# Reordering around a triangular substitution: weight splits, a norm's root, two loads and two stores

## The chip, the cores and the metric

The kernel runs on one core of a Trainium2 chip. A core has five engines, each with its own in-order instruction stream: TensorE (PE, matmuls), VectorE (DVE), ScalarE (ACT), GpSimd (POOL) and SyncE (SP, which here only issues DMAs). ACT issues DMAs too, between its own instructions. An instruction that waits holds everything behind it on its engine. The metric is the device time of one execution in microseconds (us); smaller is better.

## The reference, cut to what matters

One layer of a diffusion backbone over 1024 latent and 256 context tokens of width 1024. One input projection feeds two mixers: a neighbourhood attention of 8 heads, and a bidirectional chunked gated delta rule of 4 heads of width 128. Both are gated, concatenated and projected out.

```python
h = rmsnorm(x, g_pre) * (1.0 + scale[:, None]) + shift[:, None]
na_q, na_k, na_v, na_z, g_qkv, g_z, g_b, g_a = jnp.split(h @ w_in, IN_SPLITS, axis=-1)
o_na = neighborhood_attention(heads(na_q), heads(na_k), heads(na_v), heads(na_kc), heads(na_vc), rpb)
q, k, v = gdn_qkv(g_qkv, conv_w)                        # short conv, silu, l2norm of q and k
q, k = axial_rope(q, rope), axial_rope(k, rope)
...
a = jnp.where(pos[:, None] > pos[None, :], jnp.einsum('nbhid,nbhjd->nbhij', kb, k) * decay, 0.0)
t_inv = lax.linalg.triangular_solve(eye + a, jnp.broadcast_to(eye, a.shape),
                                    left_side=True, lower=True, unit_diagonal=True)
u = jnp.einsum('nbhij,nbhje->nbhie', t_inv, v * beta[..., None])
...
y = jnp.concatenate([o_na * jax.nn.silu(na_z), o_g * jax.nn.silu(g_z)], axis=-1) @ w_out
x = x + gate[:, None] * rmsnorm(y, g_post)
```

What the change touches is the part between: the delta rule needs, for each head, direction and chunk, the inverse of a unit triangular matrix (`t_inv`), and keys that are l2-normalised and rotated.

## The kernel before, in words

Precision: a projection is done as three matmuls for each 128-row block of the weights. A weight tile is loaded raw (`wr`), cast by ACT to a rounded high half (`wh`, L585), and the low half is the difference (`wl`, L586, on POOL, or on DVE where the tile is one of four parts and its first block is not a multiple of four). PE then does high times high, high times low and low times high (L603, L607, L608 for the form with channels as rows; L616 to L618 for the values of the attention, tiles `pv`). So PE needs `wl` a few matmuls after `wh`. The weights of the attention's values come in four parts, `nv0_0`, `nv0_2`, `nv0_4` and `nv0_6`.

Stages: up to about 75 us normalisation and the first weights; to about 430 us the convolutions and projections of the delta heads h = 0 to 3, with the projections of the attention filled in between them; to about 525 us the rest of the projections together with the merging of triangular inverses; then attention and the delta scan side by side to about 757 us; then the output projection. The program is emitted by Python generators that are stepped in turn, and a list scheduler orders the instructions of each engine; `self.order(r, name)` (L199) adds an edge without a semaphore that pins r behind another instruction of that order.

For each delta head, `qk_tok` turns q and k of the head to tokens on PE (tiles `tp`), squares them on ACT with a sum (`sq`, L1068), takes the root of the keys' sums on POOL (`rsqrt`, L216: an addition and a power, tile `rq_y_g`), scales the keys with it on DVE (`tok`, L1074) and rotates: the queries' rotary products and their sum on POOL, the keys' on DVE (L1084 to L1086). `qk_back` transposes the result back (tiles `tb`), and `delta_front` multiplies keys with keys and queries (tiles `pk`), masks on DVE and POOL (`pm`, `qe`) and stores both (`pm_dram`, `qe_dram`). A 32x32 diagonal block of the result is copied to `ab_dram` for the inversion. A second root on POOL, `rq_y_rho`, belongs to the queries and is read only in the scan.

The inverses are built in two steps. The 32x32 blocks are inverted by substitution on DVE, in the rounds m = 30 to 1 of `inv_pairs` (L1230 to L1235): each round is a product of two parts of `ab` into `tb` (L1233) and an addition back into `ab` (L1235), over 120 partitions and 2m(31-m) elements each. `inv_pairs` takes the 240 blocks of heads 0 to 2 and is stepped from the loop over the head h = 3; the last 80 blocks go through `inv_blocks` later (`ab_vv`, `tb_qh`). At the end `inv_pairs` writes the two inverses to `yd0` and `yd1` (L1241). `inv_merge` (L1266) then combines 32x32 blocks to 128x128: it loads the block factors from memory (`pmf`, L1272, two loads a head of 480 KB) and the inverted blocks (`vl`, L1285, four loads a head of 80 KB), transposes the blocks on DVE (`vx`, `vd`, `ld`, L1291 to L1293), and multiplies on PE (`tz` from `ld` and `pmf`, L1305; `tu` from ACT's copy of `tz`, L1324). Meanwhile PE has projections of the attention to do: `pq` and `pk` of head pairs 2 and 3 (`na_proj`), whose result goes to memory as a high and a low half (`sh`, `sl`, `qk_out`, both stored through SP, L680 and L681), and gates `pz` (`gate_proj`), finished by DVE (`st_z`, L704). `pq`, `pk`, `pz` and `pv` share three PSUM buffers.

## Time and profile before

| | |
|---|---|
| Three timed runs | 854.83, 853.98 and 848.80 us, median 853.98 |
| Profiled execution | 848.82 us, of which the span of the trace is 847.1; 1.7 lies around it |
| PE busy | 814.2 us, 96% of the span, mean granted clock 0.99 |
| DVE, ACT, POOL busy | 495.0 (58%), 418.0 (49%), 365.5 (43%) |
| DMA | 159.67 MB, mean 188 GB/s; SP's queue 54.0% of 16 engines' span, ACT's 5.5% |

PE is the engine to look at: nearly everything else lies beside it. So the time is PE's work plus the few places where PE stands still, and those places are read from the list of waits, from the timeline around them, and from a table of 20 us windows with PE's busy time and the clock granted to it. The profiled execution is the shortest of those known; the other two timed ones are about 5 to 6 us longer.

### The profile page before, as it was taken

The page shows a single profiled execution, that of the slowest core. Times are in us where ns is not written, and L with a number is a line of the kernel's source. Part 1 is how long each engine was busy: PE and PEld are TensorE (multiplying, and loading weights), DVE is VectorE, ACT ScalarE, POOL GpSimd, SP SyncE. Part 2 cuts the span into 40 slices and gives each one's busy share as a digit, 9 for nine tenths or more (in the row PEclk, how much of TensorE's full clock was granted, in tenths as well). Part 3 has the DMA queues.
Part 4 walks back from the last instruction along what each step waited for, and adds up shares of the span by engine and source line. Part 5 has one row for each costly group of instructions (what it writes and reads, how often), then busy time and mean ns, then how long its engine had stood idle before and what let it go on. Part 6 is the DMA issues. An engine that isn't in the chain of part 4 may idle for free.

```text
span 847.1 us, 16613 instructions
## 1 busy us (share of the span) xinstructions
PE 814.2 (96%) x6170; PEld 695.3 (82%) x6170; DVE 495.0 (58%) x988; ACT 418.0 (49%) x1097; POOL 365.5 (43%) x436
## 2 busy tenths in 40 slices
PE   8999999999999999988997999899999999999996
PEld 6688887888788878878985787799898989878885
DVE  4673455546456757699926955556566565743342
ACT  4472525654564664643214334566666666753211
POOL 0042221363482572555452103565757567835121
PEclk9999999999999999999998999999999999999999
DMA  9986442254626626733688579996967923234261
GB/s 332 341 305 213 136 138 90 79 180 161 162 75 227 197 69 230 218 110 102 202 241 239 166 223 293 392 306 181 313 186 257 250 97 128 87 125 137 99 199 50
DMA packets 86343, 159.67 MB, mean 188 GB/s; under 512 B 18405, under 2 KB 45750, under 8 KB 84086
## 3 DMA queue, kind: packets, MB, share of 16 engines
q1 hardware_dynamic: 78774, 144.94, 54.0%
q10 hardware_dynamic: 7488, 13.67, 5.5%
q8 instruction: 49, 0.80, 0.4%
q14 instruction: 32, 0.26, 0.1%
HBM read 109.51 MB, written 52.42 MB: 191 GB/s over the span
## 4 chain that ended last, share of the span: by engine, by line
PE 76%; DMA 9%; DVE 7%; POOL 3%; issue 2%; ACT 2%; SPq 0%; DVEq 0%; POOLq 0%; ACTq 0%
PE py L1550 4%; PE py L1552 3%; PE py L1551 3%; PE pz L607 3%; PE pz L608 3%; PE pz L603 3%; PE pa L1437 3%; DMA vl<-yd 2%; PE po L942 2%; PE po L937 2%; PE tr L926 2%; PE sc L905 2%; PE pa L1422 2%; PE pv L618 2%; PE pv L617 2%; PE pv L616 2%
## 5 line engine op out<-in xcount | busy, mean ns | idle before, releaser
L909 DVE CUSTOM_DVE_ANT_0 pt<-sc,gm 128x544 f32<-128x544 f32 (+1 forms) x64 | 49.4, 772 | 32.3 <-PE sc L905 28.6
L910 ACT ACTIVATE pt<-pt,nm 128x544 f32<-128x544 f32 (+1 forms) x64 | 50.5, 789 | 31.1 <-DVE nm L909 30.7
L893 POOL TENSOR_TENSOR gm<-gt,mk 128x288 f32<-128x288 f32 (+1 forms) x48 | 46.5, 972 | 21.8 <-DVE nm L909 18.6
L1412 POOL TENSOR_SCALAR kd<-kt,kd 128x128 f32<-128x128 f32 x72 | 42.7, 604 | 18.7 <-PE pa L1451 18.2
L1040 DVE SCALAR_TENSOR_TENSOR acc_v<-xp_v,cols,acc_v 128x1282 f32<-128x1282 f32 x16 | 33.1, 2068 | 26.9 <-ACT acc_v L1038 26.6
L1193 POOL TENSOR_SCALAR_AFFINE_SELECT qe<-qe 128x256 f32<-128x256 f32 x32 | 29.0, 907 | 39.8 <-DVE qe L1192 39.8
L1616 DVE TENSOR_TENSOR finv<-py,ggb 128x512 f32<-128x512 f32 (+1 forms) x17 | 10.7, 656 | 51.4 <-ACT finv L1615 43.0
L603 PE MATMUL pz<-hh,wh_gz 128*128 128x512 f32 x96 | 38.9, 405 | 0.0
L607 PE MATMUL pz<-hl,wh_gz 128*128 128x512 f32 x96 | 38.8, 405 | 0.0
L608 PE MATMUL pz<-hh,wl_gz 128*128 128x512 f32 x96 | 38.8, 404 | 0.0
L1174 ACT ACTIVATE em<-em,gc 128x128 f32<-128x128 f32 x80 | 25.5, 390 | 25.7 <-DMA em<-gc_dram 22.9
L618 PE MATMUL pv<-wl_nv,hh 128*128 128x264 f32 x104 | 30.5, 296 | 4.8 <-DVE wl_nv L586 4.8
L1189 DVE SCALAR_TENSOR_TENSOR pm<-pk,nsc,em 128x128 f32<-128x128 f32 x80 | 23.5, 342 | 18.5 <-PE pk L1182 14.6
L1418 POOL TENSOR_SCALAR vb<-v,beta 128x128 f32<-128x128 f32 x40 | 24.2, 606 | 23.0 <-DVE y L1424 13.1
L586 POOL TENSOR_TENSOR wl_gz<-wr_gz,wh_gz 128x512 fp32r<-128x512 f32 x12 | 15.5, 1290 | 37.3 <-ACT wh_gz L585 35.8
L926 PE MATMUL tr<-c,pt 128*96 128x128 f32 (+1 forms) x192 | 31.4, 273 | 0.0
L1454 DVE SCALAR_TENSOR_TENSOR s<-s,egl,pa 128x128 f32<-128x128 f32 x64 | 19.4, 342 | 20.1 <-PE pa L1451 20.1
L924 ACT COPY tcx<-tc 128x256 f32<-128x256 f32 x64 | 23.5, 367 | 15.1 <-PE tc L919 14.5
L928 ACT COPY tl<-tr 96x384 f32<-96x384 f32 (+1 forms) x64 | 30.5, 476 | 0.0
L617 PE MATMUL pv<-wh_nv,hl 128*128 128x264 f32 x104 | 30.0, 291 | 0.0
L616 PE MATMUL pv<-wh_nv,hh 128*128 128x264 f32 x104 | 29.2, 292 | 0.0
L1615 ACT ACTIVATE finv<-py 128x512 f32<-128x512 f32 x14 | 8.3, 598 | 38.7 <-PE py L1552 20.5
(469 smaller groups left out, 2859.3 us busy)
## 6 DMA issues: line engine op xcount, KB each, us to landing
wada<-in_w_ada SPq DMA_DIRECT2D x16, 512.0 KB
em<-gc_dram SPq DMA_DIRECT2D x20, 256.0 KB
pm_dram<-pm SPq DMA_DIRECT2D x20, 256.0 KB
tm_dram<-tm SPq DMA_DIRECT2D x8, 640.0 KB
kk<-qk_dram SPq DMA_DIRECT2D x16, 320.0 KB
tm<-tm_dram SPq DMA_DIRECT2D x4, 1280.0 KB
kq_dram<-kq SPq DMA_DIRECT2D x4, 1152.0 KB
kq<-kq_dram SPq DMA_DIRECT2D x4, 1152.0 KB
```

The lines of the kernel that those rows point to most:

```text
L603: r = nc.tensor.matmul(ps, wh, xh, start=(k == 0 and first), stop=False)
L607: nc.tensor.matmul(ps, wh, xl, start=False, stop=False)
L608: nc.tensor.matmul(ps, wl, xh, start=False, stop=(k == KC - 1))
L616: nc.tensor.matmul(ps, xh, wh, start=(k == 0), stop=False)
L617: nc.tensor.matmul(ps, xl, wh, start=False, stop=False)
L618: nc.tensor.matmul(ps, xh, wl, start=False, stop=(k == KC - 1))
L893: r = nc.gpsimd.tensor_tensor(self.gm[hh][:, 384 - n:384].rearrange("p (n c r) -> p n c r", c=nco, r=4), gv, self.mk[:, mo:mo + n].rearran ...
L909: nc.vector.tensor_tensor_reduce(pt[:, 384 - n:], sc[:, 512 - n:768], gm[:, 384 - n:], -1.0, 3.0e38, ALU.add, ALU.min, nm)
L910: self.last_exp = nc.scalar.activation(pt[:, 384 - n:], pt[:, 384 - n:], AF.Exp, bias=nm, scale=-1.0, accum_out=sums[:, ct, hh:hh + 1]).in ...
L926: self.pe(nc.tensor.transpose(pl[:m, rc * P:(rc + 1) * P], pt[:, 384 + (rc - 3) * m:384 + (rc - 2) * m], self.ident))
L1412: r = nc.gpsimd.tensor_scalar(kd[d], kt_[:, t, :], self.kd[:, h, d, t:t + 1], None, ALU.mult)
L1550: nc.tensor.matmul(py, mh[:, tt], wh[:, nn], start=(k == W_ORDER[0]), stop=False)
```

## The change

Six edits, all in the stretch between about 365 and 470 us.

1. `load_w`: of a weight in four parts, the third part's low half (`wl_nv0_4`) goes from POOL to DVE. The last low half and the last `st_z` are remembered by name.
2. `inv_pairs`: round m = 27 is ordered behind the last of those low halves and the last `st_z`; round m = 26 behind the last scaling of the keys of head 3 (`self.scaled`). In the loop over heads, the rounds' generator is not stepped at the fourth to sixth letter of a head's string.
3. `qk_tok`: for h = 3 the queries' two rotary sums on POOL are put off until the root of the keys is done, and are ordered behind it. The root `rho` is ordered behind the keys' root as well.
4. `inv_merge`: the loads of `vl` are issued ahead of those of `pmf`, and `pmf` is ordered behind them.
5. `qk_out`: for the head pairs 2 and 3 the high halves are stored through ACT's queue.
6. The names that the orders need are recorded (`last_root`, `split`, `gated`, `scaled`).

```diff
@@ rsqrt
-    def rsqrt(self, pool, x, n, tag, eps):
+    def rsqrt(self, pool, x, n, tag, eps, after=None):
         y = pool.tile([P, n], F32, name=f"rq_y_{tag}", tag=f"rq_y{n}")
-        self.nc.gpsimd.tensor_scalar(y, x, eps, None, ALU.add)
-        self.nc.gpsimd.tensor_tensor(y, y, bc(self.mhalf, [P, n]), ALU.pow)
+        r = self.nc.gpsimd.tensor_scalar(y, x, eps, None, ALU.add)
+        if after:
+            self.order(r, after)
+        self.last_root = self.nc.gpsimd.tensor_tensor(y, y, bc(self.mhalf, [P, n]), ALU.pow).ins.name
@@ load_w
-                (nc.vector if halves > 2 and k0 % 4 else nc.gpsimd).tensor_tensor(lo, raw, hi.bitcast(F32), ALU.subtract)
+                r = (nc.vector if halves > 2 and k0 else nc.gpsimd).tensor_tensor(lo, raw, hi.bitcast(F32), ALU.subtract)
+                self.split = r.ins.name
@@ qk_out
-        nc.sync.dma_start(self.qk_dram[0, rows, c0:c0 + n], hi.bitcast(F32))
+        (nc.scalar if p > 1 else nc.sync).dma_start(self.qk_dram[0, rows, c0:c0 + n], hi.bitcast(F32))
         nc.sync.dma_start(self.qk_dram[1, rows, c0:c0 + n], lo.bitcast(F32))
@@ gate_proj
-            nc.vector.scalar_tensor_tensor(z, z, 1.0, pz, ALU.add, ALU.mult)
+            self.gated = nc.vector.scalar_tensor_tensor(z, z, 1.0, pz, ALU.add, ALU.mult).ins.name
@@ the loop over the heads
-                for c in ("RVpppTUpB", "RppVTpUBp", "RVTpUpB", "VRppTppUB")[h]:
+                for j, c in enumerate(("RVpppTUpB", "RppVTpUBp", "RVTpUpB", "VRppTppUB")[h]):
                     step(h, c)
-                    next(blocks, None)
+                    if j < 3 or j > 5:
+                        next(blocks, None)
@@ qk_tok
             r = None if which else self.rsqrt(cv, ss, m, f"g{h}", 4 * EPS)
+            if not which:
+                for tok, rot in late:
+                    self.order(nc.gpsimd.tensor_tensor(tok, tok, rot, ALU.add), self.last_root)
...
-                    nc.vector.tensor_tensor(tok[:, :n, :], pt[:, :n, :],
-                                            bc(r[:, t0 - first:t0 - first + n].unsqueeze(2), [P, n, P]), ALU.mult)
+                    self.scaled = nc.vector.tensor_tensor(tok[:, :n, :], pt[:, :n, :],
+                                            bc(r[:, t0 - first:t0 - first + n].unsqueeze(2), [P, n, P]), ALU.mult).ins.name
...
-                    eng.tensor_tensor(tok, tok, rot, ALU.add)
+                    if which and h == 3:
+                        late.append((tok, rot))
+                    else:
+                        eng.tensor_tensor(tok, tok, rot, ALU.add)
@@ inv_pairs
+            if m == 26:
+                self.order(r, self.scaled)
+            if m == 27:
+                self.order(r, self.split)
+                self.order(r, self.gated)
@@ inv_merge
-            nc.sync.dma_start(pm[d][0:96], self.pm_dram[h][0:96, d])
...
-            nc.sync.dma_start(vl[32 * b:32 * b + 20], self.yd[g][10 * i:10 * i + 20].rearrange("t j i -> t (j i)"))
+            r = nc.sync.dma_start(vl[32 * b:32 * b + 20], self.yd[g][10 * i:10 * i + 20].rearrange("t j i -> t (j i)"))
+        for d in range(2):
+            self.order(nc.sync.dma_start(pm[d][0:96], self.pm_dram[h][0:96, d]), r.ins.name)
@@ delta_load
-            self.rho = self.rsqrt(self.cp, self.ssq.rearrange("p h t -> p (h t)"), 32, "rho", 4 * EPS)
+            self.rho = self.rsqrt(self.cp, self.ssq.rearrange("p h t -> p (h t)"), 32, "rho", 4 * EPS, self.last_root)
```

The edits move instructions, and the scheduler moves others in consequence. On DVE, in the first rounds of `inv_pairs`, before (each pair of rows that writes `tb` and then `ab` is one round; 120x216 is m = 27, 120x260 m = 26, 120x336 m = 24):

```order
239 L1233 TENSOR_TENSOR tb_3501<-ab_3500 120x216
240 L704 SCALAR_TENSOR_TENSOR st_z10_3608<-st_z10_3608,pz1_0_3583 128x512
241 L1235 TENSOR_TENSOR ab_3500<-ab_3500,tb_3501 120x2x27x4
242 L1233 TENSOR_TENSOR tb_3501<-ab_3500 120x260
243 L1235 TENSOR_TENSOR ab_3500<-ab_3500,tb_3501 120x2x26x5
244 L1233 TENSOR_TENSOR tb_3501<-ab_3500 120x300
245 L1235 TENSOR_TENSOR ab_3500<-ab_3500,tb_3501 120x2x25x6
246 L1233 TENSOR_TENSOR tb_3501<-ab_3500 120x336
247 L1235 TENSOR_TENSOR ab_3500<-ab_3500,tb_3501 120x2x24x7
248 L586 TENSOR_TENSOR wl_nv0_6_3762<-wr_nv0_6_3760,wh_nv0_6_3761 128x528
```

and the same place now (`tok3_0` are the keys of head 3, `rq_y_g3` their root):

```order
239 L707 SCALAR_TENSOR_TENSOR st_z10_3608<-st_z10_3608,pz1_0_3583 128x512
240 L588 TENSOR_TENSOR wl_nv0_4_3744<-wr_nv0_4_3742,wh_nv0_4_3743 128x528
241 L588 TENSOR_TENSOR wl_nv0_6_3750<-wr_nv0_6_3748,wh_nv0_6_3749 128x528
242 L707 SCALAR_TENSOR_TENSOR st_z11_3726<-st_z11_3726,pz1_1_3701 128x512
243 L1243 TENSOR_TENSOR tb_3501<-ab_3500 120x216
244 L1250 TENSOR_TENSOR ab_3500<-ab_3500,tb_3501 120x2x27x4
245 L1081 TENSOR_TENSOR tok3_0_0_3652<-tp3_0_0_3649,rq_y_g3_3685 128x256
246 L1081 TENSOR_TENSOR tok3_0_2_3662<-tp3_0_2_3657,rq_y_g3_3685 128x512
247 L1081 TENSOR_TENSOR tok3_0_6_3676<-tp3_0_6_3671,rq_y_g3_3685 128x512
248 L1243 TENSOR_TENSOR tb_3501<-ab_3500 120x260
```

The low half `wl_nv0_6` now stands ahead of round m = 27 and not behind m = 24; the keys' scaling, which stood behind the fifteen rounds m = 30 to 16, stands ahead of m = 26. The rounds m = 26 to 16 come behind it now. On DVE's later rows, `sl_q20`, `sl_q21` and `sl_k22`, which stood behind the last round, now stand between the last seven rounds.

On SP, from the end of head 3's front to the loads of `inv_merge`, before:

```order
218 L1200 DMA ab_dram_94<-pm_dram3_76 32x20x32 x4
219 L1241 DMA yd0_4029<-ab_3500 120x1024
220 L1241 DMA yd1_4031<-ab_3500 120x1024
221 L680 DMA qk_dram_93<-sh_q20_4303 128x512
222 L681 DMA qk_dram_93<-sl_q20_4304 128x512
223 L680 DMA qk_dram_93<-sh_q21_4385 128x512
224 L1209 DMA ab_vv_4309<-ab_dram_94 80x1024
225 L1272 DMA pmf0_0_4330<-pm_dram0_73 96x1280
226 L1272 DMA pmf0_1_4332<-pm_dram0_73 96x1280
227 L1285 DMA vl0_4334<-yd0_4029 20x1024 x4
```

and now:

```order
219 L1210 DMA ab_dram_94<-pm_dram3_76 32x20x32 x4
220 L684 DMA qk_dram_93<-sl_q20_4304 128x512
221 L684 DMA qk_dram_93<-sl_q21_4386 128x512
222 L684 DMA qk_dram_93<-sl_k22_4463 128x256
223 L1256 DMA yd0_4029<-ab_3500 120x1024
224 L1256 DMA yd1_4031<-ab_3500 120x1024
225 L1219 DMA ab_vv_4309<-ab_dram_94 80x1024
226 L684 DMA qk_dram_93<-sl_k20_4579 128x512
227 L205 DMA mk_4586<-in_masks 128x1920
228 L1299 DMA vl0_4332<-yd0_4029 20x1024 x4
229 L1301 DMA pmf0_0_4330<-pm_dram0_73 96x1280
230 L1301 DMA pmf0_1_4331<-pm_dram0_73 96x1280
```

Between `yd1` and `vl0` stood three stores of halves, `ab_vv` and both `pmf`; now `ab_vv`, one store of a half and the load of a mask (`mk`), and `pmf` follows `vl0`. On PE the first `tz` stood in the middle of `pz2_0` and now stands 20 matmuls of 512 columns later, in the middle of `pz2_1`.

On POOL, around the roots, before:

```order
140 L586 TENSOR_TENSOR wl_nv0_4_3756<-wr_nv0_4_3754,wh_nv0_4_3755 128x528
141 L1085 TENSOR_TENSOR tok3_1_6_3636<-tok3_1_6_3636,rope_1138 128x512
142 L218 TENSOR_SCALAR rq_y_rho_5542<-ssq_1140 128x32
143 L1086 TENSOR_TENSOR tok3_1_2_3621<-tok3_1_2_3621,rot3_12_3646 128x512
144 L1086 TENSOR_TENSOR tok3_1_6_3636<-tok3_1_6_3636,rot3_16_3650 128x512
145 L219 TENSOR_TENSOR rq_y_rho_5542<-rq_y_rho_5542,mhalf_67 128x32
146 L218 TENSOR_SCALAR rq_y_g3_3691<-ss3_3654 128x10
147 L1372 TENSOR_TENSOR rho2_5545<-rq_y_rho_5542 128x32
148 L219 TENSOR_TENSOR rq_y_g3_3691<-rq_y_g3_3691,mhalf_67 128x10
```

and now:

```order
140 L1092 TENSOR_TENSOR tok3_1_6_3632<-tok3_1_6_3632,rope_1138 128x512
141 L218 TENSOR_SCALAR rq_y_g3_3685<-ss3_3648 128x10
142 L221 TENSOR_TENSOR rq_y_g3_3685<-rq_y_g3_3685,mhalf_67 128x10
143 L1078 TENSOR_TENSOR tok3_1_2_3617<-tok3_1_2_3617,rot3_12_3642 128x512
144 L1078 TENSOR_TENSOR tok3_1_6_3632<-tok3_1_6_3632,rot3_16_3645 128x512
145 L218 TENSOR_SCALAR rq_y_rho_5542<-ssq_1140 128x32
146 L221 TENSOR_TENSOR rq_y_rho_5542<-rq_y_rho_5542,mhalf_67 128x32
```

The keys' root now follows the queries' rotary products directly, ahead of the queries' sums and of `rho`.

More of the change, by code (lines that the diff above doesn't have):

```diff
@@ L1052, in qk_tok @@
         nc, col = self.nc, self.col
-        toks = []
+        toks, late = [], []
         for which, acc in ((1, qa), (0, ka)):
@@ L1232, in inv_pairs @@
             t3 = tb[:, :2 * m * n].rearrange("p (g a b) -> p g a b", g=2, a=m)
-            nc.vector.tensor_tensor(t3, bc(ab[:, :, 0:m, m:m + 1], [120, 2, m, n]), bc(ab[:, :, m:m + 1, m + 1:], [120, 2, m, n]),
-                                    ALU.mult)
+            r = nc.vector.tensor_tensor(t3, bc(ab[:, :, 0:m, m:m + 1], [120, 2, m, n]),
+                                        bc(ab[:, :, m:m + 1, m + 1:], [120, 2, m, n]), ALU.mult)
+            if m == 26:
[3 more added lines that the diff above has]
+                self.order(r, self.gated)
             nc.vector.tensor_tensor(ab[:, :, 0:m, m + 1:], ab[:, :, 0:m, m + 1:], t3, ALU.add)
```

## The prediction

> **What bounds the kernel now.** PE is busy for 96% of the span, so I read first the list of waits of PE, to see where it is not. All of its waits together are some 25 us, and two of them stand out:
>
> ```profile
> PE tz L1305 <- DVE ld L1293: 5.6, 1, 5.6
> PE pv L618 <- DVE wl_nv L586: 4.8, 1, 4.8
> ```
>
> (the columns are total, times, longest). Both lie where the change is made; all others are below 2.5 us in sum and lie where the order is unchanged. So I read the timeline of PE around both. The first:
>
> ```profile
> 378.98 0.28 PE L616 MATMUL pv<-wh_nv,hh 128*128 128x264 f32 x1
> 379.10 0.28 PE L617 MATMUL pv<-wh_nv,hl 128*128 128x264 f32 x1
> 384.22 0.59 PE L618 MATMUL pv<-wl_nv,hh 128*128 128x264 f32 x1 [4.84 <-DVE wl_nv L586]
> 384.60 0.42 PE L616 MATMUL pv<-wh_nv,hh 128*128 128x264 f32 x1
> 384.82 0.42 PE L617 MATMUL pv<-wh_nv,hl 128*128 128x264 f32 x1
> ```
>
> PE stands for 4.84 us. Then the matmuls follow each other by 0.22 us and not by 0.12: the clock has fallen. Some 13 matmuls run so (until about 387.0), which is another 13 x 0.10 = 1.3 us. Gap one costs 6.1 us. The second:
>
> ```profile
> 447.11 0.40 PE L608 MATMUL pz<-hh,wl_gz 128*128 128x512 f32 x1
> 447.35 0.40 PE L603 MATMUL pz<-hh,wh_gz 128*128 128x512 f32 x1
> 453.32 2.34 PE L1305 MATMUL tz<-ld,pmf 32*32 32x32 f32 x80 [5.58 <-DVE ld L1293]
> ```
>
> and the table of windows behind it (after PE's, PEld's, DVE's, ACT's and POOL's busy time: granted clock, DMA share, GB/s):
>
> ```profile
> 456.00:458.00 2.00, 2.00 (x6) 1.52 (x6) 2.00 (x4) 1.36 (x3) 0.00 (x0) 0.50 1.03 358
> 458.00:460.00 2.00, 2.00 (x9) 1.58 (x8) 1.82 (x4) 1.97 (x6) 1.38 (x1) 0.79 0.86 262
> ```
>
> PE stands 5.58 us and then runs at half clock until about 458.7, so (458.7 - 453.3) / 2 = 2.7 us are lost besides. Gap two costs 8.3 us. Both gaps together, 14.4 us, are all that this change can win.
>
> Why gap one: the timeline of DVE.
>
> ```profile
> 380.06 0.47 DVE L1235 TENSOR_TENSOR ab<-ab,tb 120x300 f32<-120x300 f32 x1
> 380.57 1.45 DVE L1233 TENSOR_TENSOR tb<-ab 120x336 f32<-120x336 f32 x1
> 382.05 1.45 DVE L1235 TENSOR_TENSOR ab<-ab,tb 120x336 f32<-120x336 f32 x1
> 383.43 0.74 DVE L586 TENSOR_TENSOR wl_nv<-wr_nv,wh_nv 128x528 fp32r<-128x528 f32 x1
> ```
>
> The low half that PE wants stands behind substitution rounds, and these take 1.45 us where POOL works on its rotary products and sums and 0.47 where it does not.
>
> **The change part by part.** *Low halves ahead of the rounds.* How early can `wl_nv0_6` be made? ACT's timeline has its cast, and an ACT that is held later:
>
> ```profile
> 376.69 0.63 ACT L585 CAST wh_nv<-wr_nv 128x528 fp32r<-128x528 f32 x1
> ...
> 384.58 0.28 ACT L1068 ACTIVATE sq<-tp 128x128 f32<-128x128 f32 x1 [5.47 <-DVE wl_nv L586]
> ...
> 387.15 0.20 ACT L1068 ACTIVATION_READ_ACCUMULATOR sq<-tp 128x1 f32 x1
> ```
>
> The cast ends at 377.3, the subtraction takes 0.74: 378.1, or 378.8 if `wl_nv0_4`, which DVE takes over, runs late. PE needs it at 379.3. So gap one goes, -6.1, with 0.5 to 1.2 us of cover; each us beyond that comes back. In its place PE's transposes of the rotated keys stand some 60 rows earlier and can wait for DVE. No row shows this; the bounds are 0 and the 3 us by which the rope of the keys can be late, and I take +1.0.
>
> *The rounds wait for the keys' root.* ACT's squares stand behind the load of `wr_nk`, which waits for `wl_nv0_6`; they start at about 379.0 and not at 384.58, and need 387.35 - 384.58 = 2.8 us: 381.8. The root then takes POOL this long:
>
> ```profile
> 389.51 2.45 POOL L219 TENSOR_TENSOR rq_y_g<-rq_y_g,mhalf 128x10 f32<-128x10 f32 x1
> ```
>
> so DVE can scale at 381.8 + 0.3 + 2.45 = 384.5, after having stood idle for some 4 us with round m = 26 behind it. From there I count to the end of the rounds by what DVE did before:
>
> ```profile
> 385.70 0.57 DVE L1233 TENSOR_TENSOR tb<-ab 120x396 f32<-120x396 f32 x1
> ...
> 394.83 1.01 DVE L1074 TENSOR_TENSOR tok<-tp,rq_y_g 128x256 f32<-128x256 f32 x2
> ...
> 426.26 0.22 DVE L1235 TENSOR_TENSOR ab<-ab,tb 120x60 f32<-120x60 f32 x1
> ```
>
> From the scaling to the end of the last round were 426.5 - 394.8 = 31.7 us, with rounds 15 to 1. Now rounds 26 to 16 come on top: 22 to 16 took 394.8 - 385.7 = 9.1, and 26 to 23 are eight operations between 0.47 and 0.57, 4.1. With `sl_q20`, `sl_q21` and `sl_k22` pushed in (two of 0.7, one of 0.4) that is 31.7 + 9.1 + 4.1 + 1.8 = 46.7. End: 384.5 + 46.7 = 431.2, if POOL hinders no round more than before. It can: its two late sums, two more of the four subtractions for `nq2` and `nk2`, and both for `gz2` now fall beside rounds. Each can cost a round 1.45 - 0.47 = 1.0: up to 6, thus 437.2. But not every meeting does:
>
> ```profile
> 415.73 1.70 POOL L586 TENSOR_TENSOR wl_nq<-wr_nq,wh_nq 128x512 fp32r<-128x512 f32 x1 [0.24 <-ACT wh_nq L585]
> 415.77 0.50 DVE L1235 TENSOR_TENSOR ab<-ab,tb 120x336 f32<-120x336 f32 x1
> ```
>
> Here the round kept its 0.50. I take a third, 2: the rounds end at E = 433, 6.5 us later than before, within 431 and 437. [...]
>
> *The loads.* What came behind the rounds before:
>
> ```profile
> 428.75 2.60 SPq L1200 DMA_DIRECT2D ab_dram<-pm_dram  x4
> 431.45 1.15 SPq L1241 DMA_DIRECT2D yd<-ab  x2
> ```
> ```profile
> 449.82 1.25 DVE L1291 STREAM_TRANSPOSE vx<-vl 128x1024 f32<-128x1024 f32 x1 [5.39 <-DMA vl<-yd]
> ```
>
> `yd` went out 5 us behind the rounds' end, since SP stood at the copies to `ab_dram`, which wait for the last `qe` and `pm`. Those are now made many rounds earlier, so `yd` goes out at E + 0.3. From its issue to the landing of `vl` passed 449.7 - 431.5 = 18.3 us. What SP moved in that time, by size:
>
> ```profile
> pmf<-pm_dram SPq DMA_DIRECT2D x4, 480.0 KB
> yd<-ab SPq DMA_DIRECT2D x2, 480.0 KB
> vl<-yd SPq DMA_DIRECT2D x12, 80.0 KB
> qk_dram<-sh_q SPq DMA_DIRECT2D x2, 256.0 KB
> ...
> mk<-in_masks SPq DMA_DIRECT2D x1, 480.0 KB
> ab_vv<-ab_dram SPq DMA_DIRECT2D x1, 320.0 KB
> ```
>
> Two `yd`, three halves, `ab_vv`, two `pmf` and four `vl`: 960 + 768 + 320 + 960 + 320 = 3328 KB, 182 KB a us. Now two `yd`, `ab_vv`, one half, `mk` and four `vl` stand there, 2336 KB: 12.8 us. The DMA engines are full in that stretch (0.86 to 1.03 in the windows above), so the half that ACT stores meanwhile takes its place too: 256 KB, 1.4 us. With E = 433, `vl0` has landed at 433.3 + 14.2 = 447.5, and `ld` follows by 3.5 (449.8 to 453.3): 451.0. But `tz` needs `pmf` too, whose 960 KB now come behind: 5.3 us, 452.8 for the second.
>
> *PE at gap two.* It gets there at 447.75 - 6.1 + 1.0, and 20 matmuls of 0.23 (447.11 to 447.35) later in its order: 447.3. On the way it needs the buffer of `sl_q20` for `pk2_0`, whose place was here:
>
> ```profile
> 432.18 0.40 PE L603 MATMUL pk<-hh,wh_nk 128*128 128x512 f32 x1
> ```
>
> and is 427.1 now. `sl_q20` stands ahead of the last seven rounds, some 6.4 us before E (14 operations that shrink from 0.50 to 0.22, and two halves), 426.6, so this holds PE only if E is beyond 433.5, and then the wait only moves ahead of `tz`. With the first half of `tz` (0.6 us) done meanwhile, PE stands 452.8 - 447.3 - 0.6 = about 5.0 us in one or two pieces. Clock lost thereafter: between nothing and 2.7, taken as 2.0, since the pieces are shorter. The next step, `tu`, needs `vl1`, 320 KB further, and ACT's copies; I put 1.0 for it (0 to 2).
>
> *Stores through ACT.* Ten issues; an issue of SP's takes 1.15 / 2 = 0.6 by the row of `yd`. ACT is busy for 49% of the span: nothing on the path, since its waits for PE hide them; without that cover up to 6 us, of which no single wait of PE sees more than two issues, 1.2.
>
> **Sum.** -6.1 + 1.0 (gap one), -8.3 + 5.0 + 2.0 (gap two), +1.0 (`tu`): -5.4 us. Against the profiled execution, 848.8, that is 843.4. The median of the three known runs lies 5.2 above that execution, and a run to come is more like the median: 854.0 - 5.4 = 848.6 us.
>
> **Rivals.** All start from both gaps gone and the keys' wait added, -6.1 + 1.0 - 8.3 = -13.4, and differ in what comes back. *Both gaps close.* POOL hinders no round and nothing else takes DMA time: E = 431, the second `pmf` at 431.3 + 18.1 = 449.4, PE waits 1.5 at `tz`, too short to cost it clock, and 0.5 at `tu`: -13.4 + 2.0 = -11.4, 842.6. For it speaks the round of 0.50; against it those of 1.45.
>
> *Every meeting with POOL counts.* E = 436, near the upper end. PE stands 8.0 with 2.7 of clock and 1.0 at `tu`: -13.4 + 11.7 = -1.7, 852.3. Most of gap one's gain is then only carried to gap two. [...]
>
> *Slower: block factors behind blocks.* If `vl` lands no sooner behind `yd` than before, 18.3 us, because those small pieces set the time and not the KB queued ahead, then `pmf` behind it adds up to 4.9 (the 960 KB that were hidden ahead of `vl`, less a little), and with E = 437 the second `pmf` is in at 437.3 + 23.2 = 460.5: PE stands 12.6 with 2.7 of clock and 1.5 at `tu`. -13.4 + 16.8 = +3.4, 857.4. It decides from the point where the second `pmf` lands later than about 457. For it speaks that DVE becomes the bound by its idle 4 us; against it that 480 KB loads took their turn by size.
>
> **Chances.** The forecast 0.42, both gaps closed 0.18, every meeting 0.20, slower 0.20. A measurement of this kernel tells about 1% from no change, 8.5 us. Faster by more than that: nearly all of the first rival and the better third of the forecast, 0.31. Slower by more: the worse part of the last rival, with waits that I do not see, 0.12. Else 0.57. The range goes from 838.5, below the first rival, to 859, above the last, and leaves out about 2 in 10.
>
> **What would show it.** No wait of `pv` for `wl_nv` at 379; DVE idle before `tok` of head 3 until about 384.5; the last round near 433; SP issuing `yd` right behind it; the last `pmf` near 453 and PE waiting for it, not for `ld`. If the rounds end after 438, or `pmf` lands after 457, I am wrong towards slower; if PE does not wait at `tz` at all, towards faster.

## The result, and the profile after

The changed kernel takes 861.5 us (median of four runs, 860.8 to 863.7), the kernel before 852.2 beside it: ratio 1.013, interval 1.010 to 1.016. It is 1.3% slower. The forecast was 848.6 with a range of 838.5 to 859: wrong in sign, and outside the range. The profiled execution of after took 863.7 us, with a span of 862.0. Runs over 1.5% above the fastest of their kernel are left out of the ratios and mean clocks below, not of the medians: one of low halves alone (863.7 us at a clock of 0.968), one of the fourteen matmuls (875.3 at 0.961) and one of the 8 in the opening (1244.7 at 0.596).

The first part of the forecast came true. In the timeline of VectorE of after, the low half that PE waited for is made at 377.5, and the scaling of the last keys comes when the prediction had it (384.5):

```profile
377.51 1.23 DVE L588 TENSOR_TENSOR wl_nv<-wr_nv,wh_nv 128x528 fp32r<-128x528 f32 x1 [1.73 <-ACT wh_nv L587]
384.36 1.62 DVE L1081 TENSOR_TENSOR tok<-tp,rq_y_g 128x256 f32<-128x256 f32 x3 [4.24 <-POOL rq_y_g L221]
```

The list of PE's waits (total, times, longest) no longer has the 4.8 us for `wl_nv`, and the wait at `tz` is half of the 5.6 before. But there are new rows:

```profile
PE tz L1321 <- DVE ld L1309: 2.8, 1, 2.8
PE sc L905 <- DMA kk<-qk_dram: 2.2, 1, 2.2
...
PE tu L1340 <- ACT zt L1325: 2.0, 2, 1.8
...
PE pk L606 <- DVE sl_q L682: 1.8, 1, 1.8
PE tu L1360 <- ACT z L1355: 1.4, 1, 1.4
```

The rounds ended at 435.3, later than the 433 of the forecast. Five operations of the rounds took 1.55 to 1.80 instead of the 0.57 to 0.65 of operations of the same size that meet no subtraction of POOL; two of them, from the timelines of VectorE and POOL:

```profile
413.05 1.80 DVE L1243 TENSOR_TENSOR tb<-ab 120x480 f32<-120x480 f32 x1
...
422.92 1.55 DVE L1243 TENSOR_TENSOR tb<-ab 120x420 f32<-120x420 f32 x1
...
435.11 0.22 DVE L1250 TENSOR_TENSOR ab<-ab,tb 120x60 f32<-120x60 f32 x1
```
```profile
411.56 2.78 POOL L588 TENSOR_TENSOR wl_nq<-wr_nq,wh_nq 128x512 fp32r<-128x512 f32 x2 [0.15 <-ACT wh_nq L587]
...
422.44 1.58 POOL L588 TENSOR_TENSOR wl_gz<-wr_gz,wh_gz 128x512 fp32r<-128x512 f32 x1 [4.07 <-ACT wh_gz L587]
```

`yd` was then issued at 435.36, directly behind the rounds as forecast, and the first blocks landed at about 450.7. PE's timeline at the start of the merge:

```profile
451.17 0.39 PE L610 MATMUL pz<-hl,wh_gz 128*128 128x512 f32 x1
454.31 0.88 PE L1321 MATMUL tz<-ld,pmf 32*32 32x32 f32 x43 [2.75 <-DVE ld L1309]
```

Before, this `tz` started at 453.32. So up to here after is 1.0 us behind, with 22 more of the dense projection matmuls done (5.1 us of work). Attention's first scores then start 4.7 us behind, at 529.93 and not at 525.18; before first, after second:

```profile
525.18 0.39 PE L902 MATMUL sc<-kk,qh 128*128 128x256 f32 x1 [0.52 <-DVE st_z L704]
```
```profile
529.93 0.58 PE L905 MATMUL sc<-kk,qh 128*128 128x256 f32 x1 [2.18 <-DMA kk<-qk_dram]
```

Most of the rest is lost right behind that. The windows of after (third number from the end: granted clock):

```profile
520.00:524.00 4.00, 2.63 (x47) 2.42 (x46) 2.57 (x5) 3.73 (x9) 3.11 (x8) 1.00 1.15 275
524.00:528.00 4.00, 3.48 (x73) 3.12 (x70) 1.47 (x3) 1.42 (x4) 2.29 (x3) 0.63 1.05 220
528.00:532.00 4.00, 2.07 (x41) 1.79 (x45) 0.64 (x1) 0.43 (x2) 0.00 (x0) 0.50 1.01 343
540.00:544.00 4.00, 4.00 (x32) 3.67 (x30) 0.03 (x2) 2.54 (x6) 2.90 (x5) 0.50 1.01 420
552.00:556.00 4.00, 4.00 (x20) 3.03 (x19) 1.81 (x4) 1.29 (x3) 0.88 (x1) 0.50 1.01 415
```

and two of the same windows before:

```profile
540.00:544.00 4.00, 3.41 (x34) 2.58 (x33) 2.65 (x8) 1.55 (x4) 3.72 (x7) 1.00 1.01 416
552.00:556.00 4.00, 4.00 (x43) 3.83 (x39) 2.26 (x10) 2.12 (x6) 2.50 (x4) 1.00 0.99 398
```

From 525.0 to 559.2 TensorE of after has half its clock, though PE is busy for all of the windows from 532 on; before has its full clock there. The half clock begins ahead of the wait of 2.18 us for `kk`, which lasts from 527.75 to 529.93. Matmul by matmul, after is 4 to 5 us late at the start of attention, 14 at 560, and 15 at the end.

**A measure for the clock.** The mean granted clock differs from run to run of one and the same kernel. Over the 70 runs of the kernel before that were made beside the experiments it goes from 0.975 to 0.993 and the time from 857.0 to 845.2 us; a line through them falls by 5.6 us for each 0.01 (correlation -0.90). Their mean is 0.9856 and 850.2 us; after's four runs have 0.9725 and 861.9. By that line, carried a little below its lowest clock, 7 of the 12 us of difference go with the clock. For a PE that never waits an estimate from the run's 860 us is higher: 0.01 of them is 8.6 us, and at that price 0.0131 would be 11.3. Which of the two holds, and so whether anything is left for the order of the work, is what the experiments had to find out.

### The profile page after: what moved, and what is told of

The parts are those of the page before. It is cut to its first block, busy times and chain, and to the rows that moved or that the text cites. A ratio compares the mean times of both kernels' runs of the same rounds, so it can differ in the third digit from the quotient of the medians.

```text
span 862.0 us, 16612 instructions
## 1 busy us (share of the span) xinstructions
PE 831.3 (96%) x6170; PEld 709.7 (82%) x6170; DVE 495.2 (57%) x989; ACT 418.7 (49%) x1097; POOL 366.2 (42%) x435
## 4 chain that ended last, share of the span: by engine, by line
PE 73%; DVE 10%; DMA 9%; POOL 3%; issue 2%; ACT 2%; SPq 1%; ACTq 0%; POOLq 0%; DVEq 0%
PE py L1566 3%; PE py L1568 3%; PE py L1567 3%; PE pz L611 3%; PE pz L610 3%; PE pz L606 3%; PE pa L1453 3%; PE po L945 2%; PE tr L929 2%; PE sc L908 2%; PE po L940 2%; PE pa L1438 2%; PE sc L905 2%; DMA pmf<-pm_dram 2%; PE pa L1467 2%
## 5 line engine op out<-in xcount | busy, mean ns | idle before, releaser
L1330 POOL COPY tm<-ld 32x320 f32<-32x320 f32 x16 | 7.1, 447 | 49.7 <-PE tz L1354 25.7
```

## The experiments

All differ from the changed kernel or from the kernel before by the edit shown. Ratios are to runs of the kernel before on the same chip. Each expectation says what its theories are. `self.dense(p, n, after)` issues n matmuls of 128x128 into the tile `p`, behind the instruction `after` where one is named; what they write is overwritten. Such matmuls, and those of the projections, are called dense here: their rows in the traces have the form 128*128, the largest that any matmul has there.

**Four single edits to the changed kernel.** First, dense matmuls into the stretch where PE has nothing but the small merge matmuls:

```diff
+            if h == 2:
+                self.dense(pus[0]..., 5 if t0 == 0 else 4, self.tz2)   # 128x128 matmuls, ahead of head 2's last tu steps
...
+        if (p, u, hh) == (0, 0, 0):
+            self.dense(pl[:, :P], 10, self.tu2)                        # ahead of attention's first scores
```

> The changed kernel with 19 extra matmuls of 128x128 on PE whose results are overwritten: 5 and 4 ahead of the second multiplications of the merge of head 2 (tu), 10 ahead of the first scores (sc), the places where PE stands still at about 520 to 530 us behind the last dense projection. Theory 1 (the merge of the last heads has lost its cover of dense matmuls, and it is this thin stretch that halves the clock until 557 us): the clock stays near 1.00 from 526 to 560 us and the time falls to 851 to 855 us, although PE has up to 4 us more to do. Theory 2 (the clock is held down by the heavy loads of the scan's inputs, some 415 GB/s, or falls there anyhow): the half clock stays, 861 to 865 us.

Measured: 861.3 us, ratio 1.011 (1.004 to 1.017); mean clock 0.979. The time is that of Theory 2 and not of Theory 1. In the profile the clock had fallen at 517 already, in a wait of 2.5 us ahead of the added matmuls. Yet one thing in it became the key. Timeline and windows of this run:

```profile
528.98 4.63 PE L1285 MATMUL sc<-c 128*128 128x128 f32 x20
```
```profile
528.00:532.00 4.00, 4.00 (x28) 3.88 (x26) 0.98 (x2) 0.91 (x2) 0.00 (x0) 0.50 1.03 360
532.00:536.00 4.00, 4.00 (x94) 3.74 (x94) 0.73 (x2) 0.72 (x2) 0.57 (x1) 0.72 1.00 401
536.00:540.00 4.00, 4.00 (x136) 3.28 (x136) 2.46 (x6) 3.38 (x9) 3.04 (x5) 1.00 1.05 435
```

The clock came back at the end of the ten dense matmuls (20 records), and stayed for 17 us when the small ones followed. The nine ahead of them, five at 520.6 and four at 525.0 among small ones, had not brought it back.

Next, three edits undone one by one:

```diff
-            if m == 26:
-                self.order(r, self.scaled)
```

> The changed kernel without the order that puts round m = 26 behind the keys' scaling. Theory 1: the rounds end some 4 us earlier, the first tz stands 15 dense matmuls earlier in PE's order, so more of them are left for the last merges; no long half clock, 848 to 854 us. Theory 2 (the loads or stores are to blame, the rounds are not): within 3 us of the changed kernel, 858 to 865 us.

Measured: 857.1 us, ratio 1.006 (1.002 to 1.010), mean clock 0.978. The first `tz` started at 445.5, 9 us sooner than in after, but attention's first scores only 1.2 us sooner than in before, and the clock was at 0.50 from 525 to 556 all the same. The time lies between the two theories: about half of the loss is gone (1.006 against 1.013, whose intervals just touch), and the long half clock, which Theory 1 had gone, is there.

```diff
+            nc.sync.dma_start(pm[d][0:96], self.pm_dram[h][0:96, d])
         if h == 0:
...
-        for d in range(2):
-            self.order(nc.sync.dma_start(pm[d][0:96], self.pm_dram[h][0:96, d]), r.ins.name)
```

> The changed kernel with the block factors pmf loaded ahead of the blocks vl again, as before. Theory 1: the first tz starts 1 to 3 us later and PE's order is nearly the same, so the thin stretch stays: 861 to 866 us. Theory 2 (vl ahead of pmf is what costs): 851 to 856 us.

Measured: 860.0 us, ratio 1.008 (1.005 to 1.012), mean clock 0.975. It falls between the theories, nearer Theory 1. PE waited 4.6 us at `tz`; attention started 1.3 us sooner than before, and again the clock was at 0.50, from 523 to 554.

```diff
-        (nc.scalar if p > 1 else nc.sync).dma_start(self.qk_dram[0, rows, c0:c0 + n], hi.bitcast(F32))
+        nc.sync.dma_start(self.qk_dram[0, rows, c0:c0 + n], hi.bitcast(F32))
```

> The changed kernel with the high halves of head pairs 2 and 3 stored through SP again. Theory 1: the same order on PE, the thin stretch stays, 860 to 865 us. Theory 2 (stores through ACT make the attention's keys late, and the 2.2 us wait of PE for them sets off the half clock): no wait for kk and no half clock, 848 to 854 us.

Measured: 863.2 us, ratio 1.014 (1.007 to 1.022), mean clock 0.970. The wait of `sc` for `kk` is gone from the list of waits; the time is not better, as Theory 1 had it. The stores cost nothing that shows.

What follows: neither the rounds' wait nor the loads nor the stores alone carries the whole loss, and two of these kernels start attention sooner than before and are still slower, by what their clock then does.

**What sets off the half clock.** To the kernel before, one wait:

```diff
+        if h == 2:
+            for _ in range(3):
+                nc.vector.tensor_copy(z2[B], z2[B])
+            self.held = z2
...
+        if (p, u, hh) == (0, 0, 0):
+            z2 = self.held[64:128, 0]
+            nc.tensor.matmul(pc[0:64, 0:64], z2[:, 0, :], z2[:, 1, :], start=True, stop=True, tile_position=(64, 0))
```

> The kernel before, with one wait put in: behind head 2's last merge step VectorE copies z2 in place three times (64 partitions x 1280 each) and a small matmul at the head of attention's first scores reads it; its product is overwritten. Theory 1 (a wait of PE of 2 us or more among the merge's small matmuls sets off the half clock, which then lasts for some 30 us whatever is run): granted clock 0.50 in most of the windows from about 527 to 556, mean clock of the runs 0.975 or below (before: 0.985), median 858 to 866, some 2 to 4 us by the wait and 6 to 10 by the clock. Theory 2 (the half clock has nothing to do with that wait): clock 1.00 in those windows as before, mean clock 0.985, median 852 to 855, the wait alone.

Measured: 854.3 us, ratio 1.006 (1.002 to 1.010), mean clock 0.9795. Its list of waits and its windows:

```profile
PE sc L903 <- DVE z L1355: 2.2, 1, 2.2
```
```profile
528.00:532.00 4.00, 3.42 (x70) 2.96 (x71) 2.10 (x5) 0.82 (x2) 1.24 (x3) 0.50 1.00 310
536.00:540.00 4.00, 4.00 (x25) 3.41 (x24) 0.83 (x2) 1.77 (x5) 2.09 (x4) 0.50 1.02 428
540.00:544.00 4.00, 4.00 (x54) 3.27 (x53) 1.81 (x4) 1.98 (x5) 0.88 (x2) 0.89 1.02 425
```

The wait of 2.2 us brought the half clock into the kernel before, for 13.7 us; three of its four runs have a clock of 0.980 or less. The direction is Theory 1's, the size is half of it. The clock fell at 527.3, 0.9 us into the wait (526.4 to 528.6), which also held back attention's first scores.

To the changed kernel, 27 dense matmuls in all of the stretch ahead of attention:

```diff
+                if h == 2 and d == 1 and t0 == t == 0:
+                    self.dense(pz..., 8, self.tz2)
```

> The changed kernel with dense matmuls (128x128, results unused) in all of the stretch between the last gate's matmul and attention's first scores: 8 ahead of the second half of head 2's last tz step, 5 and 4 ahead of its tu steps, 10 at the head of the first scores; 27 times about 0.23 us at full clock, in time that PE otherwise waits. Theory 1 (the waits and thin matmuls of that stretch set off the half clock): clock 1.00 in the windows from 516 to 556, mean clock of the runs 0.983 or above, median 851 to 857. Theory 2 (it comes whatever runs there): clock 0.50 for 15 us or more between 516 and 556 all the same, mean clock 0.972 to 0.978, median 860 to 866 since the matmuls added then run at half clock too.

Measured: 865.3 us, ratio 1.019 (1.017 to 1.022), mean clock 0.980. The clock held as far as the added matmuls reach (529.1) and then fell twice, at 533 and at 550, among head 3's merge steps. The time is in Theory 2's range, the clock in neither's. So neither theory holds as it stands: dense work held the clock where it lay, and the fall came where it ended.

Low halves alone, on the kernel before:

```diff
-                (nc.vector if halves > 2 and k0 % 4 else nc.gpsimd).tensor_tensor(...)
+                r = (nc.vector if halves > 2 and k0 else nc.gpsimd).tensor_tensor(...)
+                self.split = r.ins.name
...
+            if m == 27:
+                self.order(r, self.split)
```

> The kernel before with the low halves of the change alone: wl_nv0_4 on VectorE and the rounds from m = 27 on behind the last low half; no other edit. Theory A (from the rounds' end the path is a chain of fixed length: yd, vl, ld, then the merge steps to attention, about 72 us from the first tz to head 3's): PE no longer waits at 379, comes to tz 6 us sooner and waits there 10 to 12 us instead of 5.6, attention starts within 1 us of before, median 850 to 855, ratio 1.000 +-0.004. Theory B (each gap of PE counts by itself): the 6 us stay gained up to the end, median 843 to 847.

Measured: 857.5 us, ratio 1.006 (1.000 to 1.012); the runs compared go from 847.8 at a clock of 0.987 to 857.8 at 0.973. At equal clock the three lie on the line of the kernel before: 2.3 us above it to 1.6 below, 0.4 above in the mean. PE's waits:

```profile
PE tz L1308 <- DVE ld L1296: 4.7, 1, 4.7
PE pv L619 <- DVE wl_nv L586: 2.4, 2, 2.2
```

Gap one is reduced from 4.8 to 2.4, and nothing of it is left at the end. Theory A's 10 to 12 us at `tz` did not come either: PE waits 4.7 there. In its profiled execution (863.7 us) the clock fell at 529.7 with no wait of 0.5 us near: small matmuls and waits of 0.3 and 0.2 us lay in the 3 us ahead.

Two edits undone together:

> The changed kernel with two of its edits undone together: no order of round m = 26 behind the keys' scaling, and pmf loaded ahead of vl as before. The low halves, the late sums, the skipped rounds and the stores by ScalarE stay. Theory A (the rounds' end sets attention's start): tz starts at 443 to 446, attention's first scores 1 to 4 us sooner than in the kernel before. By the order of work alone 847 to 850; by what its runs lose to the clock (0.974 to 0.980 in the runs of the two single edits) 851 to 857. Theory B (the two edits undone give nothing together, since PE then is bound by its own matmuls): the same as the first of them alone, 855 to 859.

Measured: 859.0 us, ratio 1.012 (1.009 to 1.015), mean clock 0.973. Theory A's gain did not come: the first `tz` started at 449.3 and not by 446, and attention's first scores at 526.0, 0.8 us later than in the kernel before. The waits moved (5.0 at `tz`, 2.5 at a `tu`), and the clock fell four times. The time is at the upper end of Theory B's range.

**Theory 3.** The trace keeps a record of the granted clock, and between 300 and 830 us each phase of half clock in it lasts a multiple of 3.41 us: 3.41, 6.83 and 34.13 in after, 3.41, 6.83 and 13.65 in the run with the wait. The phases of one profile also begin whole multiples of 3.41 us apart: those at 318.91, 383.77 and 452.03 in before 19 and 20 of them, those at 320.22, 429.45, 463.58, 507.95 and 525.02 in after 32, 10, 13 and 5. So each profile is divided here into windows of 3.41 us, carried on from its phases' borders. No idle window was needed for a fall: the clock of after fell at 429.4 and at 525.0 behind windows in which PE was busy for 1.61 and 2.90 of 3.41 us. Nor was a busy window enough to bring it back: PE was busy for 4.00 of 4.00 us at 0.50. So the matmuls of each such window, between 300 and 830 us of all 18 profiles, are weighed here by their form (rows x columns, as a part of 128 x 128) and the columns that they stream in the window; the median window is 1:

```
array work in a window     at full clock: clock fell after it    at half clock: it came back after it
below 0.11                 19 of 19                               0 of 14
0.11 to 0.23               12 of 19                               0 of 16
0.23 to 0.45               22 of 50                               10 of 54
0.45 to 0.68               15 of 100                              13 of 20
above 0.68                 0 of 2456                              45 of 45
```

PE's busy time says nearly as much of the falls: 63 of the 68 stood behind a window with PE busy for less than 2.9 us. Of the return it does not. In 122 windows of half clock PE was busy for 3.3 us or more, and the clock came back after 0 of 27 of them with array work below 0.30, 10 of 35 up to 0.45, 13 of 18 up to 0.68, and 42 of 42 above. Theory 3 is read from the table: the clock falls behind windows with little array work and comes back behind those with much. Whether the rows or the columns count more, these windows don't tell.

A 32x32 or 64x64 matmul is in PE's busy time and counts here for a sixteenth or a quarter of a dense one of as many columns. Beside head 3's merge steps the windows of before, at full clock, stand at 0.36 to 0.56 (523.7 to 544.2): at the edge, and the clock held. The ten of after at half clock stand at 0.06 to 0.45, since fewer columns pass in a window then (ten dense matmuls took 4.63 us at half clock in the first experiment and 2.50 at full clock in the run with 27), and the clock did not come back for 34 us. Whether the place of the windows' borders makes the spread from run to run is not shown: no run sets it.

The test: dense work between head 3's merge steps of the changed kernel.

```diff
+            if h == 3:
+                self.dense(pz..., 6)      # ahead of each of two tz and, alike, two tu groups; 3 ahead of each of the six last ones
```

> The changed kernel with 42 such matmuls between head 3's merge steps, which lie beside attention's opening: 6 ahead of each of its two tz and two tu groups, 3 ahead of each of the four and two of its last steps; 42 x 0.25 = 10.5 us of added work. Theory 3: the half clock that begins at 521 to 525 ends at the first or second window behind head 3's first tz, by about 535, and does not come back before 560; mean clock of the runs 0.982 or above instead of 0.9725, median 862 to 867 (the added work less some 6 by the clock). Theory 2: 0.50 up to 556 and beyond, mean clock 0.970, median 873 to 880.

Measured: 860.6 us, ratio 1.0105 (1.006 to 1.015), mean clock 0.986. With 10.5 us of useless matmuls added it is no slower than after (861.5). The windows:

```profile
520.00:524.00 4.00, 3.03 (x49) 2.89 (x47) 2.64 (x5) 3.39 (x9) 3.55 (x9) 0.86 1.13 269
524.00:528.00 4.00, 4.00 (x33) 3.74 (x32) 1.47 (x3) 1.16 (x3) 1.86 (x2) 0.50 1.05 242
528.00:532.00 4.00, 4.00 (x59) 3.53 (x58) 0.73 (x2) 0.70 (x2) 0.33 (x1) 0.78 1.02 390
532.00:536.00 4.00, 4.00 (x69) 3.77 (x67) 0.73 (x2) 3.32 (x9) 1.57 (x3) 1.00 1.04 423
552.00:556.00 4.00, 3.25 (x30) 2.51 (x29) 2.10 (x6) 1.33 (x4) 1.24 (x2) 1.00 0.99 403
```

It fell in the bare stretch, came back within two windows of 3.41 us, and stayed. Theory 3 holds for the clock; the time came out below its 862 to 867. The rival from the first experiment, that heavy loads hold the clock down, is out: full clock stands here at 423 GB/s, where after had half clock at 420.

**Is anything left for the order of the work?** The same 42 matmuls in the kernel before:

> The kernel before with the same 42 matmuls of 128x128 between head 3's merge steps that brought the changed kernel from a clock of 0.9725 to 0.986: both orders with the clock's share taken out. Theory 3 with a part for the order of work (some 3.5 to 4 us are the order's, the rest the clock's): clock 0.986 to 0.990 and a median 3 to 5 us below that of the changed kernel with the 42 (860.6), so 855.5 to 857.5. Rival (the clock was all of it, the order costs nothing): 859.5 to 861.5 at that clock.

Measured: 858.3 us, ratio 1.0101 (1.007 to 1.013), mean clock 0.990. The median lies between the two expectations. The two ratios, 1.0105 and 1.0101, are equal within their intervals (some 0.5%, 4 us), and the 2.2 us between the medians are what the 0.004 of clock between them is worth at 5.6 to 8.6 us per 0.01. So the rival is the nearer: with the clock held up the new order costs nothing that can be measured, and gains nothing, though up to 4 us either way are not excluded. The 4 us that the line of the 70 runs had left for the order are then most likely the line's error: half clock in attention's opening may cost more than the average. No run shows that by itself.

> The changed kernel without the order of round m = 26, and with the 42 matmuls. If the wait of the rounds for the keys' root is what the order costs: 2 to 3 us below 860.6, so 857.5 to 858.5, at a clock of 0.985 to 0.988. Rival (the order's part lies in the loads or the late sums): 860 to 861.

Measured: 860.8 us, ratio 1.0125 (1.008 to 1.017), mean clock 0.987: nothing gained. With the clock held up, the wait of round m = 26 for the keys' root is not what makes the changed kernel slower.

Fourteen matmuls instead of 42:

> The changed kernel with 14 such matmuls between head 3's merge steps instead of 42 (2 ahead of each of the tz and tu groups, 1 ahead of each of the last steps): 3.5 us of added work. Theory 3: it lies between the two: half clock from 521 on for 10 to 20 us instead of 34, clock 0.977 to 0.983, median 859 to 862, so nothing won or lost by it. Rival (the share of work must pass a bound and 14 do not reach it): clock 0.9725 and 864 to 867.

Measured: 859.9 us, ratio 1.011 (1.007 to 1.015), mean clock 0.981: half clock from 523 to 537 in the profile, between the two, as Theory 3 had it.

**Can it be turned to a gain?** Dense matmuls into the waits of the kernel before, 18 ahead of the first `tz` and 8 in the opening:

> The kernel before, its order unchanged, with 26 matmuls of 128x128 whose results are overwritten, only where PE waited in its profile: 18 ahead of the first tz (it waits 5.6 us there), 2 ahead of attention's first scores, 6 ahead of the second half of head 3's last tz step (it waits 1.5 there); 0.25 us each. Theory 3 (the clock falls after a window of some 3.4 us in which little of the array works, and head 3's merge keeps it down; before stands at the edge of that): no half clock at 452 to 459, fewer runs with one from 524 on; mean clock of the runs 0.990 to 0.994 (before: 0.985), median 3 to 5 us below the median of before in the same call. Theory 2 (the clock's falls have nothing to do with how much of the array works): clock 0.985, median the same as before or 1 us above.

Measured: 856.5 us, ratio 1.007 (1.004 to 1.009). This run tests nothing at the first `tz`: the 18 depend on nothing late and were placed far ahead, in time that PE had no lack of work in:

```profile
417.99 4.18 PE L1270 MATMUL tz<-c 128*128 128x128 f32 x36
```

The same on the kernel with the low halves alone:

> The kernel before with the low halves alone and the same 26 matmuls as in the first of these runs. If gap one's 6 us only move to the wait ahead of the first tz, its time at equal clock is that of the first of these runs, within 1.5 us; Theory 3 has its mean clock at 0.988 to 0.993 (low halves alone: 0.979 in its three runs) and its median at 845 to 849. Theory 2: clock 0.979, median 853 to 858.

Measured: 857.1 us, ratio 1.0085 (1.005 to 1.012), for the same reason: its 18 stand at 415.5. Its mean clock was 0.986 instead of the 0.979 without the 26.

Only the 8 in the opening:

> The same without the 18 ahead of the first tz: only the 8 in attention's opening. Theory 3: the half clock at 452 to 459 stays, that from 524 on comes in fewer runs; mean clock 0.987 to 0.990, median 1 to 3 us below before. Theory 2: as before.

Measured: 849.9 us, ratio 0.9996 (0.997 to 1.002), mean clock 0.988, none of the eleven runs compared below 0.985, where the 70 of before go down to 0.975. The clock is better as expected, the time is not; an estimate from 8 x 0.25 = 2 us is that the eight matmuls use the gain up.

And the matmuls at the first `tz`, now made to read `vl` so that they can't run sooner:

> The kernel before with 12 matmuls of 128x128 that read vl, directly ahead of the first tz (vl has landed 3.5 us before ld is made, and they take 12 x 0.25 = 3.0), and the 8 in attention's opening. Theory 3: the two windows of half clock at 452 to 459 become one or none; clock 0.989 to 0.992 and a median 1 to 3 us below before in the same call. Rival (the matmuls run at half clock themselves, since the empty window lies ahead of them, and end after ld is made): the same as before or up to 3 us slower.

Measured: 852.9 us, ratio 1.003 (1.000 to 1.005). The timeline and a window:

```profile
451.65 4.60 PE L1271 MATMUL tz<-vl,c 128*128 128x128 f32 x20 [5.56 <-DMA vl<-yd]
```
```profile
452.00:456.00 4.00, 4.00 (x20) 4.00 (x20) 3.63 (x7) 1.78 (x4) 0.88 (x2) 0.50 0.79 203
```

The rival holds: the empty window lies ahead of them (PE was busy for 0.35 us from 448 to 452), they run at half clock themselves, and end after `ld` is made. No version beat the kernel before.

## Why the prediction was wrong

*Gap one goes, -6.1 + 1.0.* Right: no wait for `wl_nv`, the low half at 377.5, and the wait for the rotated keys at 1.2 us.

*The rounds end at E = 433.* 435.3. The scaling at 384.36 was met; the meetings with POOL were undersized, and the rest of the count was some 1.8 too long. Five operations beside POOL's subtractions lost 0.96 to 1.15 each, 5.1 in all, and the round m = 26, beside POOL's late sums, 0.8 (1.22 instead of 0.43), where the term had 2 of a possible 6. The single row of 0.50, on which the prediction took a third of the 6, misled for this term: the rows of after show 5.9 lost, though E itself came out about midway between 437, which all of the 6 give, and the forecast's 433.

*The loads.* `yd` right behind the rounds: right. `vl0` 15.3 us behind it instead of 14.2, and PE waited at `tz` for `ld`, not for `pmf`; small errors.

*PE comes to `tz` at 447.3.* It came at 451.6. The wait of `pk2_0` for `sl_q` was foreseen as one that "only moves ahead of `tz`". It didn't only move: behind the 1.8 us of waiting the clock was at half from 429.4 to 432.9 as well, so part of the head start was spent there. The first rival had called a wait of 1.5 us too short to cost clock, as one of 1.54 us was in before (it ended at 534.5, and the clock from 532 to 536 was 1.00).

*"20 matmuls later in its order", counted as gain.* This is the step of the sum that failed. `tz` itself was forecast at 452.8, a mere 0.5 us sooner than before; nearly all of the -5.4 was dense work that is done ahead of `tz` and so is missing behind it. That work was not saved but borrowed. From the first `tz` to head 3's the merge took 72 us before and after (453.3 to 525.9, 454.3 to 526.3), with 22 dense matmuls fewer to lay beside it. At the end of head 2 none was left: the last projection matmul stood at 518.8, not at 523.4. PE waited 1.4 us among small matmuls, its clock fell at 525.0, it waited 2.2 us more, and the head start was gone at attention's start.

*No term for the clock behind the merge.* This is where the 12 us came from. Head 3's first `tz` came 0.4 us later than before, the end of its merge 13.0 us later; the last `tu` of before and after (first and last start):

```profile
L1346 PE MATMUL tu<-z,xo x80: 218/219/268, 476.1 to 541.3; 64*64 64x64 f32 x80
```
```profile
L1362 PE MATMUL tu<-z,xo x80: 218/218/366, 478.9 to 554.3; 64*64 64x64 f32 x80
```

The time follows this point and not attention's start: in all 18 profiles the span ends 305.7 to 311.1 us behind it, while attention's first scores come at anything from 522.1 to 536.6. The prediction priced the clock only behind PE's waits, by 1.3 and 2.7 us. That a stretch with a busy PE can lose its clock for 34 us was in no term and no rival; in the profile of before there was no such row. All four runs of after have a clock below 0.98 (0.969 to 0.975), and 8 of the 70 of before; 42 dense matmuls put back into the merge brought it to 0.986. That it was the borrowed matmuls that had held the clock fits this, but isn't shown: with two edits undone the last projection matmul stood at 523.7, as late as before, and the clock fell at 527.9 all the same.

*Stores through ACT, 0.* Right. *Slower* by more than 8.5 us had 0.12, and its rival another mechanism (block factors landing after 457); PE's list of waits has none for `pmf`, so that rival was wrong too.

What stays open: which of the edits thins the opening most. Each of the kernels between before and after had a mean clock between 0.970 and 0.979 when its opening was left alone, with 3 to 10 runs each, and these don't tell them apart. Nor was it tried to hold back real projection matmuls for the opening.

## What to carry to other kernels

Work that is done ahead of a wait is only a gain if the stretch behind that wait was bound by PE; where a chain of fixed length runs there, it is borrowed from it, so follow the sum to the place where the engine next runs dry. Before moving dense matmuls away from small-tile ones, look at what they do for the clock: the stretch of small matmuls here stood at half clock for 34.1 us in after and for two windows of 3.41 us with 42 dense ones laid into it, though PE read as busy either way. When the mean granted clock varies between runs of one kernel, compare kernels at equal clock, best by holding it up in both.

## What the runs showed of the hardware

- Half clock for 34.1 us, with PE busy for 4.00 of 4.00 us in each window from 532 to 560. In one run ten 128x128 matmuls in a row ended the half clock of this stretch; in five profiles of kernels without such matmuls it ended 4 to 7 us behind head 3's merge, in two others (stores through SP, the wait put in) during the merge, after 17.1 and 13.7 us.
- Windows of 3.41 us in which PE was busy for 1.61 us (a wait of 1.8 us among projection matmuls) and for 2.90 us (small matmuls) were followed by half clock; of 2456 windows with more than 0.68 of the median's array work none was.
- Among windows of half clock in which PE was busy for 3.3 us or more, full clock came back after 42 of 42 with array work above 0.68 and 0 of 27 below 0.30.
- The mean clock of a run of one kernel on one core went from 0.975 to 0.993, worth 12 us of 850.
- 42 matmuls of 128x128 without use, 10.5 us of work, cost the changed kernel nothing (860.6 against 861.5), the kernel before 9 us (858.3 against 849.1).
- Operations of the rounds beside a subtraction of POOL took 1.55 to 1.80 us instead of 0.57 to 0.65, in five of the meetings of after.
